# S5's direct terms placed by float32r matmuls of two parts, and the parameter work in seven parts per set

## The chip, the cores and the metric

The kernel runs on one core of one Trainium2 chip. The metric is the device time of one execution in microseconds (us), as the median of several runs. TensorE is called PE here (PEld is its weight load), VectorE is DVE, ScalarE is ACT, GpSimd is POOL and SyncE, which issues nearly all transfers, is SP. The granted TensorE clock is a share of 2.4 GHz: 1.00 is 2.4 GHz, 0.50 is 1.2 GHz.

## The reference, cut to what matters

Two two-layer networks run one after the other on 256 tokens of width 1024. Two stages matter here: the mixture of experts of the first network's second layer, and the S5 mixer that follows it.

```python
def hierarchical_moe(h, w_group, b_group, w_expert, b_expert, w_gate, w_up, w_down):   # 32 experts, top 2
    ...
        hb = jax.nn.silu(xb @ w_gate[e]) * (xb @ w_up[e])     # w_gate, w_up: 1024 x 512, float32
        return hb @ w_down[e]                                 # 512 x 1024
    ...

def s5_mixer(x, lam_re, lam_im, log_dt, b_re, b_im, c_re, c_im, d_skip, w_glu, w_out):
    ...
    a_re = mag * jnp.cos(li * dt)
    a_im = mag * jnp.sin(li * dt)
    ...
    bb_re = coef_re[..., None] * br - coef_im[..., None] * bi
    ...
    _, _, h_re, h_im = lax.associative_scan(
        _complex_linear_combine, (a_re_t, a_im_t, bu_re, bu_im), axis=1)
    y = (jnp.einsum('bsgp,gcp->bsgc', h_re, c_re.astype(f32))
         - jnp.einsum('bsgp,gcp->bsgc', h_im, c_im.astype(f32)))
    y = y + d_skip.astype(f32).reshape(N_GROUPS_2, SSM_GROUP) * u
    ...
```

S5 has 64 groups of 16 channels with 64 states. The kernel takes four time steps at once. What reaches an output from inputs of the same four steps does not go through the scan; these are the direct terms, products of C, powers of the decay and B, with `d_skip` on the diagonal.

## The kernel before

**The sets.** `moe(layer, ...)` goes through the 32 experts in eight sets of four (`qd` 0 to 7; set 1 is `qd` 0, set 8 is `qd` 7). All 25.2 MB of a set's float32 weights come from HBM through a ring of tiles of 1 MB (eight of them from set 3 of the second expert layer on), issued by SP in program order. A tile can be filled again only when the matmuls that read it are done. A set's order is: 16 tiles of gate and up weights in pairs (64 matmuls, L981), SiLU (L1000) and the product `hh` (L1001, DVE), four transposes (L1006), a copy to `ht` (L1008, ACT), and then 32 down matmuls (L1031) on eight tiles. The results are scaled into two float32r parts `y` (L1034 on ACT, L1035 on DVE) and spread back to the tokens (`back`, L1043), and DVE adds them (L1055). In every second set PE also gathers the next two sets' tokens (`gather`, L933). Set 7 adds six DVE operations on whole rows (L96 of `renew` and L989). Set 8 takes the down product in column pieces of 512, 256, 128 and 128 and makes the norm's moments as it goes (L308, L309); `norm_end` follows, with L331 on ACT as its first pass over the rows, and S5 begins.

**The parameter work.** S5's parameters need no tokens, so `s5_prepare` makes them beside the experts of the second expert layer. It is a generator; `moe` calls `next(stages)` at six places of each of the sets 1 to 7: after each half of the gate and up matmuls, after `hh`, after the second and the fourth quarter of the down matmuls, and after the adds. `stages` waits `NY` such calls, changes the ring, waits `N0` more and then runs `s5_prepare`. In set 8 whatever is left is run at once, ahead of the down matmuls. For each half of the groups (32) the parts are: `pair` of B (transposes L1368, copies `pr`), `bb` (L1388 to L1393), `W` (L1400 to L1404) with transposes L1410 to `BL`, `pair` of C (L1366), `CL` (L1419 to L1423) and then, twice, a `K` of 16 groups: matmuls L1432, copies L1434, the diagonal (L1436, L1438) and the placing. At the end come the tables `tab` of cosines and sines by doubling (L1470 to L1475, with `cmul` at L1242 to L1247, and L1483), which eight transfers (L96) copy into ring tiles.

**The placing.** `K` holds 16 x 64 numbers for each of 16 groups, in 16 partitions. Eight float32 matmuls (L1446) with slices of a 0/1 matrix `sel` of 16 rows move them to their place among 128 partitions; ACT copies the result to `KT` (L1449). The placing is done four times.

**What sets the order.** The program is written in this order, and the framework's scheduler then fixes one static order for every engine; buffers are handed over by semaphores. Each engine works through its own list strictly in order, so an instruction that waits holds up all behind it on its engine.

Of the kernel before, what the change touches and what calls it, by code (L numbers as in the profile page):

```python
# [8 lines left out]
F32 = mybir.dt.float32  # L9
F32R = mybir.dt.float32r  # L10
# [4 lines left out]
OP = mybir.AluOpType  # L15
# [20 lines left out]
GI = 1  # L36
NY = 12
NS = 1
# [6 lines left out]
EARLY = 1, 0  # L45
N0 = 4
FAST = (0, 1), (0, 1)
# [26 lines left out]
class Net:  # L74
# [707 lines left out]
    def moe(self, layer, rows, stages=()):  # L782
# [10 lines left out]
        with ExitStack() as ph:  # L793
# [170 lines left out]
            for qd in range(8):  # L964
# [57 lines left out]
                for i in range(4):  # L1022
                    v.tensor_copy(gs[32 * i:32 * i + 32], o[32 * i:32 * i + 32, i:i + 1])
                ob = [self.bank() for _ in range(2)]
                y = [[B.tile([128, 512], F32R, name=f"y{i}{j}", bufs=1) for j in range(2)] for i in range(2)]
# [223 lines left out]
    def s5_prepare(self):  # L1249
# [8 lines left out]
        with ExitStack() as es:  # L1258
# [80 lines left out]
            v.tensor_copy(dT, p[:16, :64])  # L1339
            sel = S.tile([16, 196], F32, name="sel")  # L1340
            nc.gpsimd.memset(sel, 0.0)
            v.tensor_copy(sel[:, 67:131:4], self.ident[:16, :16])
# [36 lines left out]
            for g0 in (0, H):  # L1379
# [46 lines left out]
                for q0 in range(g0 // 2, g0 // 2 + 16, 8):  # L1426
                    K = S.tile([16, 16, 4, 16], F32, name="K", tag="W")
                    for h8 in range(2):
                        p = self.bank("tp")
                        for g in range(8):  # L1430
# [6 lines left out]
                                    dT[:, q0 * 2:q0 * 2 + 16, None].to_broadcast([16, 16, 16]), op=OP.mult)  # L1437
                    v.tensor_tensor(K[:, :, 0, :], K[:, :, 0, :], dd, op=OP.add)  # L1438
                    yield
                    p = self.bank("tp")  # L1440
                    po = p.rearrange("p (q i c) -> p q i c", q=8, i=4)
                    Kg = K.rearrange("p (q g) n c -> p g q n c", g=2)
                    n = 0
                    for j in range(4):
                        for g in range(2):
                            nc.tensor.matmul(po[:, :, j:4, :], lhsT=sel[:, 67 - 64 * g - j:195 - 64 * g - j], rhs=Kg[:, g, :, 0:4 - j, :],  # L1446
                                             start=n == 0, stop=n == 7)
                            n += 1
                    a.copy(KT[:, q0:q0 + 8, :], p.rearrange("p (q m) -> p q m", q=8))  # L1449
# [15 lines left out]
            m = 1  # L1465
            while m < 64:
# [10 lines left out]
                if m < 64:  # L1477
                    w2 = [R.tile([128, H], F32, name=f"ww{m}{i}") for i in range(2)]
                    self.cmul(R, w2, wp, wp, [128, H], "cm")
                    wp = w2  # L1480
                else:
                    yield
# [498 lines left out]
    def stages0(self):  # L1981

        self.folds[1]()
        for _ in range(33):
            yield
# [66 lines left out]
```

## Time and profile before

| what | value |
|---|---|
| median of 3 runs (1853.5 to 1857.93) | 1855.04 us |
| profiled execution, its own time | 1861.03 us |
| its span, first to last instruction | 1859.1 us |
| mean granted TensorE clock | 0.938 |
| PE busy | 1583.7 us (85%) |
| DVE busy | 844.3 us (45%) |
| ACT busy | 500.0 us (27%) |
| read from HBM | 526.49 MB, 284 GB/s over the span |

The profile is one execution; it is 0.3% above the median. Busy shares are means over stages with different limits. The second expert layer lies between about 640 and 1230 us of the span, S5 after it.

### The profile page before, as it was taken

The page shows a single profiled execution, that of the slowest core. Times are in us where ns is not written, and L with a number is a line of the kernel's source. Part 1 is how long each engine was busy: PE and PEld are TensorE (multiplying, and loading weights), DVE is VectorE, ACT ScalarE, POOL GpSimd, SP SyncE. Part 2 cuts the span into 40 slices and gives each one's busy share as a digit, 9 for nine tenths or more (in the row PEclk, how much of TensorE's full clock was granted, in tenths as well). Part 3 has the DMA queues.
Part 4 walks back from the last instruction along what each step waited for, and adds up shares of the span by engine and source line. Part 5 has one row for each costly group of instructions (what it writes and reads, how often), then busy time and mean ns, then how long its engine had stood idle before and what let it go on. Part 6 is the DMA issues. An engine that isn't in the chain of part 4 may idle for free.

```text
span 1859.1 us, 24869 instructions
## 1 busy us (share of the span) xinstructions
PE 1583.7 (85%) x10036; PEld 1025.0 (55%) x10044; DVE 844.3 (45%) x1786; ACT 500.0 (27%) x807; POOL 123.8 (7%) x205
## 2 busy tenths in 40 slices
PE   7898777877786999787678779777999999999997
PEld 6773321322222995132223323256989998879997
DVE  5962011210312963014331442278775657785655
ACT  4721000000001632000110100033554445655441
POOL 3000000000100301000000010012100100300100
PEclk9988989998899999898997987879999999999999
DMA  9358999999999857999998999975745543435530
GB/s 305 148 210 354 420 420 420 419 420 420 410 420 384 308 211 293 420 411 390 409 377 344 375 369 362 367 141 176 252 138 199 185 142 108 159 136 182 185 111 23
DMA packets 150519, 535.55 MB, mean 288 GB/s; under 512 B 23141, under 2 KB 35686, under 8 KB 120698
## 3 DMA queue, kind: packets, MB, share of 16 engines
q1 hardware_dynamic: 148226, 532.04, 75.5%
q0 software_dynamic: 1856, 1.75, 0.4%
q8 instruction: 81, 1.33, 0.3%
q14 instruction: 44, 0.36, 0.1%
q10 hardware_dynamic: 312, 0.07, 0.0%
HBM read 526.49 MB, written 1.05 MB: 284 GB/s over the span
## 4 chain that ended last, share of the span: by engine, by line
PE 38%; DMA 13%; DVE 6%; ACT 2%; issue 1%; POOL 1%; SPq 0%; DVEq 0%; ACTq 0%; POOLq 0%
DMA raw<-in_moe_w_up 9%; PE mm L503 5%; PE mm L502 5%; PE mm L504 5%; PE mm L1031 4%; PE tp L503 3%; PE tp L502 3%; PE tp L504 3%; PE mm L981 3%; DMA raw<-in_moe_w_gate 2%; DMA raw<-in_moe_w_down 2%; PE tp L1446 2%; PE tp L933 1%; PE tp L1432 1%; DVE h L96 0%
## 5 line engine op out<-in xcount | busy, mean ns | idle before, releaser
L981 PE MATMUL mm<-raw,xg 128*32 128x512 f32 x2048 | 367.9, 684 | 152.7 <-DMA raw<-in_moe_w_up 86.9
L295 DVE TENSOR_TENSOR wlo<-raw,whi 128x1024 fp32r<-128x1024 f32 (+3 forms) x265 | 282.3, 1081 | 170.5 <-ACT whi L294 169.6
L981 PEld LDWEIGHTS mm<-raw,xg 128*32 128x32 f32 x2048 | 79.3, 121 | 424.7 <-DMA raw<-in_moe_w_up 153.4
L294 ACT CAST whi<-raw 128x1024 fp32r<-128x1024 f32 (+3 forms) x265 | 239.1, 919 | 244.9 <-PE mm L504 103.3
L1031 PE MATMUL mm<-raw,ht 128*32 128x512 f32 (+2 forms) x1120 | 205.8, 603 | 14.7 <-DMA raw<-in_moe_w_down 11.1
L1001 DVE TENSOR_TENSOR hh<-hh,mm 128x512 f32<-128x512 f32 x16 | 11.0, 688 | 423.4 <-PE mm L981 399.2
L502 PE MATMUL mm<-whi,f 128*128 128x512 f32 (+3 forms) x432 | 150.0, 347 | 0.0
L503 PE MATMUL mm<-wlo,f 128*128 128x512 f32 (+3 forms) x432 | 149.9, 347 | 0.0
L504 PE MATMUL mm<-whi,f 128*128 128x512 f32 (+3 forms) x432 | 149.1, 346 | 0.0
L503 PE MATMUL tp<-f,whi 128*128 128x256 f32 x512 | 145.1, 284 | 2.5 <-DVE f L419 2.5
L502 PE MATMUL tp<-f,whi 128*128 128x256 f32 x512 | 145.0, 284 | 0.4 <-ACT f L413 0.4
L504 PE MATMUL tp<-f,wlo 128*128 128x256 f32 x512 | 144.8, 283 | 0.0
L1031 PEld LDWEIGHTS mm<-raw,ht 128*32 128x32 f32 x1120 | 51.6, 117 | 124.4 <-issue 88.2
L1000 ACT ACTIVATE hh<-mm 128x512 f32<-128x512 f32 x16 | 9.6, 597 | 390.3 <-PE mm L981 359.9
L503 PEld LDWEIGHTS tp<-f,whi 128*128 128x128 f32 x512 | 98.3, 192 | 3.2 <-DVE f L419 3.2
L502 PEld LDWEIGHTS tp<-f,whi 128*128 128x128 f32 x512 | 98.1, 192 | 1.3 <-ACT f L413 0.9
L504 PEld LDWEIGHTS tp<-f,wlo 128*128 128x128 f32 x512 | 98.3, 192 | 0.0
L503 PE MATMUL mm<-xl,whi 128*128 128x272 f32 (+2 forms) x320 | 93.1, 292 | 0.9 <-DVE xl L419 0.5
L502 PE MATMUL mm<-xh,whi 128*128 128x272 f32 (+2 forms) x320 | 91.7, 292 | 0.6 <-ACT yg L674 0.4
L504 PE MATMUL mm<-xh,wlo 128*128 128x272 f32 (+2 forms) x320 | 92.0, 289 | 0.0
L502 PEld LDWEIGHTS mm<-whi,f 128*128 128x128 f32 x432 | 81.8, 189 | 10.3
L504 PEld LDWEIGHTS mm<-whi,f 128*128 128x128 f32 x432 | 81.5, 189 | 10.1 <-DVE f L419 0.2
(613 smaller groups left out, 2385.7 us busy)
## 6 DMA issues: line engine op xcount, KB each, us to landing
raw<-in_moe_w_gate SPq DMA_DIRECT2D x128, 1024.0 KB, 16.5
raw<-in_moe_w_up SPq DMA_DIRECT2D x128, 1024.0 KB, 19.9
raw<-in_moe_w_down SPq DMA_DIRECT2D x120, 1024.0 KB, 18.1
raw<-in_w_ff SPq DMA_DIRECT2D x64, 1024.0 KB, 5.0
raw<-in_sc_w_in SPq DMA_DIRECT2D x12, 1024.0 KB, 12.4
raw<-in_lru_w_in SPq DMA_DIRECT2D x8, 1024.0 KB, 13.9
raw<-in_ssm_w_glu SPq DMA_DIRECT2D x8, 1024.0 KB, 10.8
raw<-in_moe_w_down SPq DMA_DIRECT2D x12, 512.0 KB, 13.3
```

What stands on the lines that cost most here:

```text
L294: f(self.nc.scalar.copy)(hi, src)
L295: f(self.nc.vector.tensor_tensor)(lo, src, hi.bitcast(F32), op=OP.subtract)
L502: mm(out, lhsT=lh, rhs=rh, start=first, stop=False, skip_group_check=shared)
L503: mm(out, lhsT=lh, rhs=rl, start=False, stop=False, skip_group_check=shared)
L504: mm(out, lhsT=ll, rhs=rh, start=False, stop=last, skip_group_check=shared)
L933: nc.tensor.matmul(o, lhsT=hk[n][:, k, :], rhs=P[n], start=n == 0, stop=n == 1)
L981: nc.tensor.matmul(gu[m][i * 32:(i + 1) * 32, :], lhsT=xg[hf][:, k, c], rhs=wgu[hf * n + part][m][i][:, k % (4 // n), :], start=hf == 0 an ...
L1000: a.activation(hh, gu[0], AF.Silu)
L1001: v.tensor_tensor(hh, hh, gu[1], op=OP.mult)
L1031: nc.tensor.matmul(o[e * 32:(e + 1) * 32, :], lhsT=ht[:, j, e * 32:(e + 1) * 32], rhs=w[e], start=j == 0, stop=j == 3)
L1432: nc.tensor.matmul(p[:16, g * 64:(g + 1) * 64], lhsT=bb[0][:, gg - g0, :], rhs=CL[:, gg, 0:4, :].rearrange("p n c -> p (n c)"), start=True ...
L1446: nc.tensor.matmul(po[:, :, j:4, :], lhsT=sel[:, 67 - 64 * g - j:195 - 64 * g - j], rhs=Kg[:, g, :, 0:4 - j, :], start=n == 0, stop=n == 7)
```

## The change

1. `s5_prepare`'s placing. `sel` becomes float32r. `K` is copied to a float32r tile `Kh` by ACT; DVE makes the remainders `Kl = K - Kh` in two halves of eight groups. The eight float32 matmuls over all columns become eight float32r matmuls of `Kh` over all columns and two times eight of `Kl` over half the columns, all into the same PSUM bank: 24 instead of 8. The old placing read `K` itself, and the new one reads `Kh` and `Kl`.
2. `moe` calls `next(stages)` at a seventh place, ahead of the down matmuls, in both expert layers.
3. The counts are moved with it: `NY` 12 to 14 (the ring still changes at the start of set 3), `N0` 4 to 3 (`s5_prepare` begins ahead of set 3's down matmuls and not after the last of them), and the first layer's count 33 to 38.
4. The tables are made in three parts and not in one. With 32 calls left for `s5_prepare`, and not 26, its last K and all its tables come before set 8.

```diff
-NY = 12
+NY = 14
...
-N0 = 4
+N0 = 3
...
                 for i in range(4):
                     v.tensor_copy(gs[32 * i:32 * i + 32], o[32 * i:32 * i + 32, i:i + 1])
+                if qd < 7:
+                    next(stages, None)
                 ob = [self.bank() for _ in range(2)]
...
-            sel = S.tile([16, 196], F32, name="sel")
-            nc.gpsimd.memset(sel, 0.0)
+            sel = S.tile([16, 196], F32R, name="sel")
+            nc.gpsimd.memset(sel.bitcast(F32), 0.0)
...
+                    Kh = S.tile([16, 16, 4, 16], F32R, name="Kh")
+                    a.copy(Kh, K)
+                    parts = [(Kh, slice(0, 8))]
+                    for i, tag in enumerate(("pr1", "bb1")):
+                        Kl, e = S.tile([16, 8, 4, 16], F32R, name="Kl", tag=tag), slice(8 * i, 8 * i + 8)
+                        v.tensor_tensor(Kl, K[:, e], Kh[:, e].bitcast(F32), op=OP.subtract)
+                        parts.append((Kl, slice(4 * i, 4 * i + 4)))
                     yield
...
-                    Kg = K.rearrange("p (q g) n c -> p g q n c", g=2)
-                    n = 0
-                    for j in range(4):
-                        for g in range(2):
-                            nc.tensor.matmul(po[:, :, j:4, :], lhsT=sel[:, 67 - 64 * g - j:195 - 64 * g - j], rhs=Kg[:, g, :, 0:4 - j, :],
-                                             start=n == 0, stop=n == 7)
-                            n += 1
+                    for t, e in parts:
+                        t = t.rearrange("p (q g) n c -> p g q n c", g=2)
+                        for j in range(4):
+                            for g in range(2):
+                                nc.tensor.matmul(po[:, e, j:4, :], lhsT=sel[:, 67 - 64 * g - j:195 - 64 * g - j], rhs=t[:, g, :, 0:4 - j, :],
+                                                 start=e == slice(0, 8) and j + g == 0, stop=e.start == 4 and j + g == 4)
...
-                else:
+                if m > 8:
                     yield
...
-        for _ in range(33):
+        for _ in range(38):
```

Up to set 3 of the second expert layer every engine's list is the same as before, and SP's list of transfers is the same throughout. Line numbers in the changed kernel are 2 higher from L1024 on and 8 to 10 higher behind the placing: L1031 is L1033 there, L1446 is L1455, L1470 is L1478. Three places show what moved.

PE in set 5, before: a piece of the down matmuls (L1031, four at a time) with the products of K (L1432) and the placing (L1446) between them.

```order
L1432 MATMUL tp<-CL,bb_6918 16x64 x2
L1446 MATMUL tp<-K,sel 128x512 x2
L1031 MATMUL mm<-raw,ht 32x512 x4
L1446 MATMUL tp<-K,sel 128x8x48 x2
L1031 MATMUL mm<-raw,ht 32x512 x4
L1446 MATMUL tp<-K,sel 128x8x32 x2
L1446 MATMUL tp<-K,sel 128x8x16 x2
L1432 MATMUL tp<-CL,bb_6918 16x64 x14
L1031 MATMUL mm<-raw,ht 32x512 x4
L1432 MATMUL tp<-CL,bb_6918 16x64 x2
```

PE in set 5 of the changed kernel, from the last placing instructions to the end of the down matmuls (L1033), with the transposes for the second half's B (L1370) and BL (L1412).

```order
L1455 MATMUL tp<-Kl,sel 128x4x32 x2
L1455 MATMUL tp<-Kl,sel 128x4x16 x2
L1033 MATMUL mm<-raw,ht 32x512 x12
L1370 MATMUL tp<-ident,raw 128x32 x16
L1033 MATMUL mm<-raw,ht 32x512 x12
L1412 MATMUL tp<-ident,W 128x128 x8
L1033 MATMUL mm<-raw,ht 32x512 x4
L1412 MATMUL tp<-ident,W 128x128 x2
L1033 MATMUL mm<-raw,ht 32x512 x4
L1412 MATMUL tp<-ident,W 128x128 x6
```

Two placings with both their products stood among set 5's down matmuls; now one whole placing stands ahead of them and none among them. The other placings went to the end of set 4 and the start of set 5, into set 6's down matmuls, and into set 7's gate and up matmuls.

PE at set 8, before: the last placing stands between the small matmuls behind the transposes of `hh` and the first down matmuls.

```order
L1017 MATMUL tp<-gt,P_7662 128x4
L1446 MATMUL tp<-K,sel 128x512 x2
L1446 MATMUL tp<-K,sel 128x8x48 x2
L1446 MATMUL tp<-K,sel 128x8x32 x2
L1446 MATMUL tp<-K,sel 128x8x16 x2
L1031 MATMUL mm<-raw,ht 32x512 x16
L1031 MATMUL mm<-raw,ht 32x256 x2
```

PE at set 8 of the changed kernel, the same place.

```order
L1014 MATMUL tp<-ident,P_7830 128x128
L1017 MATMUL tp<-gt,P_7828 128x4
L1017 MATMUL tp<-gt,P_7830 128x4
L1033 MATMUL mm<-raw,ht 32x512 x16
L1033 MATMUL mm<-raw,ht 32x256 x2
L1045 MATMUL mm<-y_8372,pt 128x512 x2
```

Nothing stands between `hh` and the down matmuls of set 8 any more.

DVE in set 8, before: the last doubling of the tables, with set 8's second `y` (L1035) and its adds and moments (L308, L309) among them.

```order
L308 SCALAR_TENSOR_TENSOR h_64<-h_64,mm 128x512
L1471 TENSOR_TENSOR tt<-tab,ww_8273 128x1024
L1473 TENSOR_TENSOR tab<-tab,ww_8272 128x32x32
L1472 TENSOR_TENSOR tab<-tab,tt 128x32x32
L1035 SCALAR_TENSOR_TENSOR y_8181<-mm,gs,y_8180 128x256
L1474 TENSOR_TENSOR tt<-tab,ww_8273 128x1024
L309 BN_STATS bst_8341<-h_64 128x6
L1475 TENSOR_TENSOR tab<-tab,tt 128x32x32
L308 SCALAR_TENSOR_TENSOR h_65<-h_65,mm 128x512
L1483 TENSOR_SCALAR tab<-tab 128x2048
```

DVE in the changed kernel, where the tables end: the `hh` behind them (L1001) is that of set 7.

```order
L1481 TENSOR_TENSOR tab<-tab,ww_8152 128x32x32
L1479 TENSOR_TENSOR tt<-tab,ww_8153 128x1024
L1480 TENSOR_TENSOR tab<-tab,tt 128x32x32
L1482 TENSOR_TENSOR tt<-tab,ww_8153 128x1024
L1483 TENSOR_TENSOR tab<-tab,tt 128x32x32
L1491 TENSOR_SCALAR tab<-tab 128x2048
L1001 TENSOR_TENSOR hh<-hh,mm 128x512
L1020 CAST pt<-tp 128x256
```

All the tables, and set 7's six row operations ahead of them, are now in front of set 7's `hh` in DVE's list, and set 8's `hh`, `y` and moments have nothing of the parameter work among them.

## Rows read from the trace of the kernel before

**Rows 1.** Busy time by stretch: sets 4 to 7, cut at last up weights.

Columns: stretch, its length, then per engine busy us and (x instructions), the granted clock, the DMA share, GB/s.

```profile
912.80:979.30 66.50, 50.57 (x322) 21.62 (x322) 22.31 (x42) 8.55 (x15) 0.98 (x2) 0.97 0.99 386
979.30:1051.00 71.70, 61.02 (x322) 23.95 (x322) 19.60 (x37) 5.00 (x8) 0.00 (x0) 0.86 0.90 346
1051.00:1118.00 67.00, 52.66 (x322) 21.96 (x322) 29.26 (x46) 8.57 (x15) 6.94 (x8) 0.92 0.97 381
1118.00:1185.40 67.40, 54.67 (x294) 19.88 (x294) 9.66 (x19) 3.14 (x5) 0.00 (x0) 0.83 0.96 375
```

**Rows 2.** Busy time by stretch: where the transfers fall behind.

```profile
944.00:958.00 14.00, 9.03 (x56) 3.39 (x60) 12.48 (x21) 1.24 (x3) 0.00 (x0) 0.88 0.85 297
1006.00:1030.00 24.00, 24.00 (x140) 11.42 (x142) 8.33 (x13) 2.55 (x4) 0.00 (x0) 0.89 0.65 218
1090.00:1096.00 6.00, 6.00 (x42) 1.52 (x44) 5.83 (x8) 0.00 (x0) 2.69 (x2) 0.72 0.37 105
1144.00:1158.00 14.00, 13.63 (x96) 7.85 (x98) 5.85 (x9) 1.96 (x3) 0.00 (x0) 0.86 0.70 247
```

**Rows 3.** Groups of PE's instructions, 860 to 1230 us: records, busy, mean ns.

```profile
L1446 PE MATMUL tp<-K,sel 16*128 16x512 f32 (+3 forms) x64 | 29.7, 625 | 2.9 <-DVE K L1438 2.8 <-ACT ht L1008 0.2
...
L933 PE MATMUL tp<-P,h 128*128 128x256 f32 x64 | 18.3, 429 | 1.0 <-ACT BL L1412 1.0
L1432 PE MATMUL tp<-CL,bb 128*16 128x64 f32 x128 | 11.0, 256 | 0.3 <-ACT ht L1008 0.2
L1410 PE MATMUL tp<-ident,W 128*128 128x128 f32 x32 | 4.8, 283 | 0.3 <-ACT ht L1008 0.2
L1366 PE MATMUL tp<-ident,raw 32*64 32x32 f32 x128 | 4.7, 219 | 0.0
```

**Rows 4.** Timeline of PE in sets 1 and 4: start, duration, instruction.

```profile
742.07 8.08 PE L1031 MATMUL mm<-raw,ht 128*32 128x512 f32 x64 [0.19 <-ACT ht L1008]
...
917.38 1.91 PE L1031 MATMUL mm<-raw,ht 128*32 128x512 f32 x8
...
952.44 5.83 PE L981 MATMUL mm<-raw,xg 128*32 128x512 f32 x48
```

**Rows 5.** Timeline of DVE in sets 4 and 6.

```profile
944.82 0.69 DVE L1421 TENSOR_TENSOR CL<-pr,p 128x512 f32<-128x512 f32 x1
...
949.64 1.40 DVE L1035 SCALAR_TENSOR_TENSOR y<-mm,gs,y 128x512 fp32r<-128x512 f32 x2
...
1083.09 1.23 DVE L96 TENSOR_TENSOR h<-h,gb 128x1024 f32<-128x1024 f32 x1
```

**Rows 6.** Busy time by stretch: set 5's clock, and the end of weights.

```profile
960.00:990.00 30.00, 18.27 (x123) 6.13 (x124) 3.65 (x10) 1.18 (x2) 0.00 (x0) 1.00 1.03 410
992.00:1006.00 14.00, 14.00 (x37) 5.25 (x37) 0.00 (x0) 0.58 (x1) 0.00 (x0) 0.50 1.03 410
...
1207.00:1208.00 1.00, 0.00 (x0) 0.00 (x0) 1.00 (x4) 0.00 (x0) 0.00 (x0) 1.00 0.35 82
```

**Rows 7.** Timeline of all engines, from set 8's down matmuls into S5.

```profile
1191.21 7.78 PE L1446 MATMUL tp<-K,sel 16*128 16x512 f32 x16 [0.17 <-ACT ht L1008]
...
1199.38 0.23 DVE L1470 TENSOR_TENSOR tab<-tab,wp 128x32 f32<-128x32 f32 x1 [6.52 <-POOL tab L1463]
...
1204.57 0.69 ACT L1034 ACTIVATE y<-mm,gs 128x512 fp32r<-128x512 f32 x1 [4.96 <-DVE ww L1243]
...
1209.63 0.75 DVE L1035 SCALAR_TENSOR_TENSOR y<-mm,gs,y 128x512 fp32r<-128x512 f32 x1
...
1220.70 1.21 DVE L1483 TENSOR_SCALAR tab<-tab 128x2048 f32<-128x2048 f32 x1
...
1222.82 1.94 PE L1031 MATMUL mm<-raw,ht 128*32 128x128 f32 x32 [2.33 <-DVE y L1035]
...
1229.59 0.81 ACT L331 ACTIVATE h<-h,bmv 128x512 f32<-128x512 f32 x1 [4.32 <-DVE bmv L330]
...
1241.62 7.70 PE L1518 MATMUL mm<-f,place 128*128 128x512 f32 x32 [1.92 <-ACT f L413]
```

## Prediction, as put on record before the changed kernel ran

> **What bounds the kernel now.** The page shows PE at 85% and DVE at 45%, means over stages with different limits, so I went to the stage that the change touches, the second expert layer, and cut it by sets. [rows 1] cut it where a set's last up weights have landed (T4 = 912.8, T5 = 979.3, T6 = 1051.0, T7 = 1118.05, T8 = 1185.4). In the undisturbed stretch of [rows 6] the transfers run at 410 GB/s, and 25.17 MB at that rate take 61.4 us. The four steps took 66.5, 71.7, 67.0 and 67.4, so 27.0 us were lost. The same loss is seen where it happens, in [rows 2]: a stretch of length d at rate r loses d(1 - r/410), which gives 3.9, 11.2, 4.5 and 5.6, together 25.2 us. I use the second number. In three of the four stretches PE is busy all or nearly all the time: the ring's tiles are not given back because PE is not yet done. In the first PE waits, 9.0 of 14, and DVE is busy 12.5.
>
> How late PE may be follows from set 4. PE began to read set 5's first pair at 952.44, T4 + 39.6 [rows 4], and a pair takes about 2.0, so the tiles came back at T4 + 41.6 and the stretch lost 3.9. The transfers therefore run on if the first pair is given back by about T + 37.7.
>
> The second place is the tail. The last weights have all but landed at 1207.4 (82 GB/s in the last microsecond, [rows 6]), yet the last 32 down matmul records begin at 1222.82, and L331, the end of the norm's chain, at 1229.59 [rows 7]. Between them stand the last placing (7.78) ahead of the down matmuls, and the tables on DVE from 1199.38 to 1221.91, with set 8's `y` in their midst (1209.63, though ACT's half was ready at 1205.26).
>
> **The price of a placing.** Before: 29.7/4 = 7.4 us of PE [rows 3], mostly at half clock. After: 24 matmuls over 2560 + 2560 columns. The nearest float32r row is L1518, 32 matmuls of 512 columns in 7.70, 0.24 each [rows 7]; by columns that is 2.4 us. From above, the small products of L1432 (64 matmuls, 11.0/64 = 0.17 each, [rows 3]) give 24 x 0.17 = 4.1; and if float32r cost as much a column as the float32 placing, it would be 14.8. Below 2.4 nothing speaks for. I take 3 at full clock, since the columns per matmul lie between these rows, and 6 at half. New beside it: `Kh` on ACT, and two `Kl` on DVE, of about a `pr` or CL operation each (0.60 a piece by the eight CL operations from 944.82 to 949.64, [rows 5]), 2 us of a chain that only the `Kl` matmuls wait for.
>
> **The boundaries, set by set, at full clock.** From T to the first down matmul 4.6 us pass (917.38 in [rows 4]). Eight groups of four down matmuls in one run take 8.08, about 1.0 each; a group that stands alone takes 1.9 [rows 4]. So every piece of parameter work put between them costs 0.9 more than itself. From the start of the second-to-last `y` to the next pair's read it is 2.8 (949.64 to 952.44).
>
> Set 4 now holds the rest of BL (half of 4.8/2, 1.2), C's pair (4.7/2 = 2.35), the gather (18.3/2 = 9.15), one K's products (11.0/4 = 2.75), a third of a placing (1.2), and its down matmuls in six single groups and a double one (14.3). With 4.6 + 2.8 + 2.0 that is 40.4, so 2.7 us late against 3.9: C comes earlier, so its chain on DVE (three copies and twelve CL operations at 0.6, 9) is now under the gather, and no longer at the end.
>
> Set 5 held two placings and seven cuts at half clock. It now holds one placing (3, ahead of its down matmuls; its `Kl` stand ahead of `hh` on DVE, so PE does not wait for them), B's pair (2.35), BL (2.4) and four runs of down matmuls (11.6). That is 24 with the first 4.6; DVE's chain is longer: from the pair's end at T + 14, 2 for `pr`, then 24 operations of at most 0.6 (bb and two W), so `y` at T + 30.4, the next pair back at 35.2. It fits by 2.5 at full clock. I leave 1.5 us for the clock.
>
> Set 6 gets C's pair, K's products and a placing: 4.6 + 2.35, then CL until T + 17, products 2.75, K's copies and `Kh` 2, four single groups 7.6, Kl 1.7, a part of the gather 2, then 2.8 + 2.0: about 40, and part of the gather and the last placing stand among set 7's first gate and up matmuls. I take 3 late against 4.5.
>
> Set 7 has no parameter work in its down matmuls: 4.6 + 8.1 + 2.8 + 2.0 = 17.5, 20 us to spare against 37.7. That pays for DVE, whose list now has the six row operations (1.23 each, [rows 5]) and all tables (1199.38 to 1221.91, at most 22.5, some of it set 8's own, [rows 7]) ahead of set 7's `hh`. I put their start at T6 + 45, an estimate: the next pair back at 40, and some 5 for what is left of the gather. They end at T6 + 75 at the latest, when T7 is at T6 + 64.4 and `hh` is wanted at T7 + 2. So PE's transposes of `hh`, and all down matmuls behind them, wait up to 8.6 us, within the 20; 5.6 us are gained.
>
> After: 2.7 + 1.5 + 3 + 0 = 7.2 lost instead of 25.2, a gain of **18**. From one side all 25.2 come back; from the other, sets 5 and 6 at half clock lose about 10 and 8, which leaves a gain of 4.
>
> **The tail.** With the placing gone the down matmuls begin at 1191.2 (set 8's own scale) and not at 1199, a gain of 7.7, and without the tables `y` follows ACT's half (1205.26) and does not wait until 1209.63, 4.4: 12.1 together. Further waits for `y` would give more, but the weights land no earlier than T8 + 22.0, and from the last matmuls to L331 it is 6.8: T8 + 29.1 at best against T8 + 44.2, 15.1. Taken: **13.5**. What is late next is the last weights themselves. S5's first steps wait for the norm and for `tab`, whose transfers (behind the weights on SP) can now start when the weights end, so they stay hidden. Calls in the first layer cost nothing: its lists are the same, and the weights cover the ring's change as before.
>
> **Sum.** 18 + 13.5 = 31.5 us, from 1859.1 to 1827.6 of span. The execution profiled is 0.3% over the median, for which I keep the difference: 1855.04 - 31.5 = **1823.5**.
>
> **Rivals.** (a) The placings are cheap but the boundaries stay late, since the clock stays at half there: PE at 0.50 in 992 to 1006 while it was busy throughout, with the 16-row placing in its list, and 1.00 in 960 to 990 with 18.3 of 30 busy [rows 6]. The parameter work's many small pieces are still there, and if they bring the half clock as the placing did, only 0 to 8 of the 25.2 return: 1855 - 13.5 - 4 = 1837.5. The Trainium skill (TensorE: Matmul & The Clock Gate, section "HAM oscillation — how this bites in real kernels") has it that pauses of the matmuls for transfers send the clock to half, and by that a shorter placing would bring more of it, and the time would be this rival's; these two stretches show the reverse, so the rule adds nothing to its chance. (b) More comes back than I count, all stalls and the best tail: 1855 - 40 = 1815. (c) Slower: the half clock reaches through sets 4 to 6 whole. Then what PE does after T doubles: set 4 from 33 to 66, set 5 from 22 to 44, set 6 by 15; beyond T + 37.7 that is some 35, 8 and 17, 60 us lost instead of 25.2, and the tail at its lower end gives 12: 1878. It decides from a loss of 37 (25.2 + 12). Against it: in [rows 1] whole steps show 0.83 to 0.97. (d) The placing is no cheaper, as float32r costs what float32 does by column: 14.8 a placing instead of 3: sets 4, 5 and 6 are then late by 6.6, 9.3 and 14.8, 30.7 against 25.2, and with the tail the gain is 8, 1847. L1518's row speaks against it.
>
> **How the numbers follow.** Forecast (a gain of 22 to 37) 0.66; (b) 0.10; (a) 0.13; (d) 0.04; within 0.2%, which is about what a measurement of this kernel can tell from no change (1851.3 to 1858.7), 0.03; slower, by (c) or by DVE's list in set 7 passing its 20 us of room, 0.04. Range 1813 to 1840: it takes in (b) and (a) and leaves (c), (d) and no change out.
>
> **What would show it.** Right: 24 placing matmuls in about 3 us; T5 - T4 to T8 - T7 at 62 to 65, with no stretch like 1006 to 1030; set 7's `hh` some us after its last up matmul, with no dip of the transfers behind it; in set 8 the first down matmuls within 2 us of `hh`, and L331 at T8 + 29 to 32. Wrong: granted clock near 0.5 behind T5 and T6 with dips as before; the placing above 6; tables that end far behind T7; or S5 waiting for `tab`.

## The result, and the profile after

The changed kernel takes 1835.0 us (median of 4 runs, 1833.4 to 1836.7) against 1854.6 (4 runs, 1853.5 to 1857.9): a ratio of 0.9884, 95% interval 0.9856 to 0.9912. It is faster by 19.6 us where 31.5 were forecast; the time lies in the range, on its slower side. The execution profiled took 1836.65; its span is 1834.9, against 1859.1 before:

```profile
span 1834.9 us, 24946 instructions
```

The windows view of the changed kernel, first the steps T4 to T8 (T4 = 913.9, T5 = 980.0, T6 = 1044.6, T7 = 1110.5, T8 = 1172.0), then the stretches in which the transfers fall off. Columns: stretch, its length, busy time of PE, PE's weight loads, DVE, ACT and POOL, granted clock, DMA share, GB/s.

```profile
913.90:980.00 66.10, 56.60 (x402) 28.84 (x402) 24.59 (x45) 9.66 (x15) 0.98 (x2) 0.97 1.01 392
980.00:1044.60 64.60, 46.40 (x269) 18.70 (x269) 19.48 (x38) 7.08 (x12) 0.00 (x0) 0.87 0.97 379
1044.60:1110.50 65.90, 56.25 (x418) 29.82 (x418) 44.73 (x112) 9.27 (x14) 7.68 (x10) 1.00 1.00 391
1110.50:1172.00 61.50, 39.64 (x214) 10.91 (x215) 14.52 (x21) 2.56 (x4) 0.00 (x0) 0.89 1.03 408
952.00:966.00 14.00, 13.42 (x124) 7.59 (x122) 3.23 (x6) 1.63 (x2) 0.00 (x0) 1.00 0.93 348
1012.00:1024.00 12.00, 9.98 (x70) 4.06 (x72) 6.24 (x11) 2.34 (x4) 0.00 (x0) 1.00 0.74 242
1084.00:1100.00 16.00, 16.00 (x100) 8.68 (x103) 13.27 (x22) 2.76 (x4) 5.75 (x6) 1.00 0.90 334
```

Against [rows 1] the steps fell from 66.5, 71.7, 67.0 and 67.4 to 66.1, 64.6, 65.9 and 61.5. By d(1 - r/410), as for [rows 2], the last three lines lose 2.1, 4.9 and 3.0; behind T7 there is no such stretch.

The timeline of the changed kernel at set 7's `hh`, at the last up weights of set 8, and in the tail (start, length, engine, line; in brackets the wait ahead of it and what ended it):

```profile
1118.32 1.23 DVE L1491 TENSOR_SCALAR tab<-tab 128x2048 f32<-128x2048 f32 x1
1119.46 0.68 DVE L1001 TENSOR_TENSOR hh<-hh,mm 128x512 f32<-128x512 f32 x1
...
1171.97 1.91 PE L981 MATMUL mm<-raw,xg 128*32 128x512 f32 x12 [1.51 <-DMA raw<-in_moe_w_up]
...
1176.21 2.22 PE L1033 MATMUL mm<-raw,ht 128*32 128x512 f32 x4 [0.17 <-ACT ht L1008]
...
1182.81 6.42 PE L1033 MATMUL mm<-raw,ht 128*32 128x512 f32 x30 [1.66 <-DMA raw<-in_moe_w_down]
...
1203.43 0.81 ACT L331 ACTIVATE h<-h,bmv 128x512 f32<-128x512 f32 x1 [3.94 <-DVE bmv L330]
```

Set 7's `hh` stands behind the last of the tables, at T7 + 8.9. L331 comes at T8 + 31.5, before at T8 + 44.2 [rows 7]. The first down matmuls wait for `ht` alone, the later ones for their weights.

### The profile page after: what moved, and what is told of

Read it like the earlier page. It is cut to its first block, busy times and chain, and to the rows that moved or that the text cites. A ratio compares the mean times of both kernels' runs of the same rounds, so it can differ in the third digit from the quotient of the medians.

```text
span 1834.9 us, 24946 instructions
## 1 busy us (share of the span) xinstructions
PE 1550.8 (85%) x10068; PEld 1023.2 (56%) x10076; DVE 850.7 (46%) x1794; ACT 504.5 (27%) x811; POOL 123.7 (7%) x205
## 3 DMA queue, kind: packets, MB, share of 16 engines
q0 software_dynamic: 1856, 1.75, 0.4%
## 5 line engine op out<-in xcount | busy, mean ns | idle before, releaser
L981 PE MATMUL mm<-raw,xg 128*32 128x512 f32 x2048 | 360.7, 660 | 153.0 <-DMA raw<-in_moe_w_up 89.3
L1033 PE MATMUL mm<-raw,ht 128*32 128x512 f32 (+2 forms) x1120 | 193.8, 588 | 17.1 <-DMA raw<-in_moe_w_down 16.2
L1001 DVE TENSOR_TENSOR hh<-hh,mm 128x512 f32<-128x512 f32 x16 | 11.0, 687 | 412.1 <-PE mm L981 387.8
L1033 PEld LDWEIGHTS mm<-raw,ht 128*32 128x32 f32 x1120 | 47.8, 113 | 125.5 <-issue 82.9
## 6 DMA issues: line engine op xcount, KB each, us to landing
raw<-in_ssm_w_glu SPq DMA_DIRECT2D x8, 1024.0 KB, 10.8
```

Of the source, the lines that this page charges most:

```text
L981: nc.tensor.matmul(gu[m][i * 32:(i + 1) * 32, :], lhsT=xg[hf][:, k, c], rhs=wgu[hf * n + part][m][i][:, k % (4 // n), :], start=hf == 0 an ...
L1001: v.tensor_tensor(hh, hh, gu[1], op=OP.mult)
L1033: nc.tensor.matmul(o[e * 32:(e + 1) * 32, :], lhsT=ht[:, j, e * 32:(e + 1) * 32], rhs=w[e], start=j == 0, stop=j == 3)
```

## The experiments

For every profiled execution the same three numbers were read from its trace. **Loss**: over stretches of 2 us between the `hh` of one set and the next, the sum of 2(1 - r/410) where r is under 395 GB/s. **Half clock**: from the granted clock of the same stretches, from set 4's `hh` to set 8's. **Tail**: from set 8's `hh` to L331. The first two rows are two executions of one kernel, and so are the third, fourth and fifth of one order of instructions. Medians stand with the ratio to the kernel before on the same chip. The three numbers belong to the one execution profiled, which can lie several us off its kernel's median (moving alone: 1846.8 against 1841.9; control to B early: 1832.5 against 1838.1).

| kernel | median, ratio (95% interval) | loss of sets 4, 5, 6, 7 (sum) | half clock | tail |
|---|---|---|---|---|
| before | 1854.6 | 3.9, 11.3, 4.5, 5.9 (25.6) | 60 | 40.6 |
| before again | profiled execution 1847.5 | 5.0, 10.1, 4.5, 1.5 (21.1) | 48 | 38.5 |
| changed | 1835.0, 0.9884 (0.9856 to 0.9912) | 2.7, 4.9, 3.1, 0.1 (10.8) | 34 | 29.4 |
| changed, again | 1834.6, 0.9889 (0.9861 to 0.9916) | 2.5, 2.8, 8.9, 0.3 (14.5) | 67 | 27.5 |
| changed, tables held for set 8 | 1831.5, 0.9846 (0.9802 to 0.9890) | 2.9, 1.1, 3.6, 0.1 (7.7) | 27 | 29.5 |
| float32r placing alone | 1851.2, 0.9975 (0.9958 to 0.9992) | 4.9, 11.5, 5.1, 0.2 (21.7) | 51 | 37.5 |
| moving alone | 1841.9, 0.9926 (0.9897 to 0.9954) | 3.3, 6.3, 13.5, 0.2 (23.3) | 61 | 31.2 |
| upper part alone | 1834.1, 0.9879 (0.9853 to 0.9906) | 4.1, 1.3, 6.8, 0.2 (12.4) | 49 | 30.0 |
| dummy matmuls | 1831.6, 0.9854 (0.9819 to 0.9890) | 2.9, 1.9, 6.9, 0.2 (11.9) | 31 | 29.3 |
| N0 at 6 | 1840.8, 0.9904 (0.9871 to 0.9936) | 4.9, 0.2, 10.9, 0.2 (16.2) | 34 | 31.0 |
| N0 at 7 | 1846.2, 0.9940 (0.9915 to 0.9966) | 4.6, 10.2, 3.7, 2.7 (21.2) | 51 | 30.9 |
| B early | 1833.2, 0.9889 (0.9863 to 0.9915) | 2.8, 1.5, 4.9, 0.2 (9.4) | 27 | 30.6 |
| control to B early | 1838.1, 0.9923 (0.9893 to 0.9953) | 2.3, 4.8, 5.0, 0.1 (12.2) | 20 | 30.0 |
| B early, N0 at 2 | 1840.6, 0.9928 (0.9903 to 0.9954) | 15.6, 0.4, 2.2, 0.2 (18.4) | 41 | 29.5 |

**The two halves of the change.** First the float32r placing in the order of before:

```diff
-            sel = S.tile([16, 196], F32, name="sel")
+            sel = S.tile([16, 196], F32R, name="sel")
...
+                    Kh = S.tile([16, 16, 4, 16], F32R, name="Kh")
+                    a.copy(Kh, K)
...
```

> The kernel before with the float32r placing alone; calls, counts and tables as before. Theory (placing and moving gain in different places): a placing takes 3.8 us as in the changed kernel and not 7.4; the two placings in set 5 and the one in set 7 no longer hold up the next set's pairs, so the steps T5 to T6 and T7 to T8 (71.7 and 67.4) come to about 66 and 64, T4 to T5 and T6 to T7 stay at 66 to 67; the tail keeps its tables on DVE, whose end then binds, so T8 to L331 falls by no more than 4 (44.2 to 40 or more). Sum 10 to 13: about 1843, a ratio of 0.994. Rival 1 (the type of the matmuls is all): the steps come out as in the changed kernel and the tail too, 1835 to 1838. Rival 2 (the moving is all): the steps stay as before, 1851 or more.

It gains 0.25%, some 4 us: less than the theory's 10 to 13, and as little as its second rival (the moving is all, 1851 or more). The tail and set 7 gained little more than the second execution of before shows of itself, and set 5, with two placings, lost as much as ever. Its timeline and windows in set 5:

```profile
991.73 1.18 PE L1453 MATMUL tp<-Kh,sel 16*128 16x512 f32 x2 [2.45 <-ACT Kh L1440]
992.84 3.63 PE L1031 MATMUL mm<-raw,ht 128*32 128x512 f32 x8
```

```profile
990.00:1002.00 12.00, 10.27 (x27) 3.81 (x27) 2.16 (x5) 1.04 (x1) 0.00 (x0) 0.57 1.03 410
1006.00:1034.00 28.00, 25.58 (x166) 11.52 (x163) 14.93 (x24) 4.28 (x6) 0.00 (x0) 0.88 0.70 242
```

The shorter placing waits for its own new chain (`Kh`, 2.45), and the clock is at half from 992 to 1002 with no float32 placing in the list.

Then all the rest of the change with the float32 placing:

```diff
-                    Kh = S.tile([16, 16, 4, 16], F32R, name="Kh")
...
+                    Kg = K.rearrange("p (q g) n c -> p g q n c", g=2)
...
```

> The changed kernel with the float32 placing of before (8 matmuls, 7.4 us at full or half clock); the seventh call, the counts and the three parts of the tables as in the changed kernel. Theory: the tail gains all it gained in the changed kernel (T8 to L331 at 31 to 32, before 44.2), since no placing and no table is left in set 8; the boundaries gain little, for four placings cost 3.6 more each in sets 4 to 7, so T4 to T8 sums to 265 to 273 (258.1 in the changed kernel, 272.6 before). Time 1839 to 1847, a ratio of about 0.993. Rival 1 (the float32 placing brings half clock wherever it stands): granted clock near 0.5 behind each placing and T4 to T8 at 275 or more, 1850 or more. Rival 2 (moving is all): 1835 to 1837.

It comes out as the theory had it, 1841.9, T4 to T8 in 270.3, L331 at T8 + 33.2. The two halves add up to 17 (4 + 13) of the 20 us, with intervals of 3 and 5 us to either side. In the execution profiled, what float32r brings in the new order is mostly set 6, which loses 13.5 here at half clock; how much of that is the placing's is not shown, since this set of the changed kernel lost 3.1, 8.9 and 3.6 in three executions. The first of these windows is set 6's boundary, the second the stretch behind it; the rows are the first placing, at full clock:

```profile
1046.00:1070.00 24.00, 19.43 (x159) 10.21 (x152) 13.80 (x26) 1.78 (x3) 0.97 (x2) 0.66 1.03 409
1080.00:1114.00 34.00, 33.77 (x192) 16.76 (x191) 25.05 (x70) 4.11 (x7) 6.18 (x8) 0.90 0.73 251
```

```profile
943.18 1.12 PE L1448 MATMUL tp<-K,sel 16*128 16x512 f32 x2
...
946.07 1.77 PE L1448 MATMUL tp<-K,sel 16*128 16x512 f32 x4
...
950.79 1.99 PE L1448 MATMUL tp<-K,sel 16*128 16x384 f32 x8
...
954.56 0.48 PE L1448 MATMUL tp<-K,sel 16*128 16x128 f32 x2
```

That is 5.4 us in four pieces, not 7.4.

**The kernel before a second time.**

> The kernel before, unchanged, profiled a second time. The first profile's execution took 1861.03 us, 6.4 over the median of 1854.6, and the forecast took its terms from it. If that excess lay where the terms were read (sets 4 to 7 of the second expert layer, their half-clock stretches), the steps T4 to T8, 272.6 us in the first profile, come out some 4 to 6 us shorter here at a time near 1854 to 1856, the most of it in T5 to T6 (71.7). If the excess lay elsewhere, the steps sum to 272 +- 1.5 again and the rest of the program is shorter.

T4 to T8 took 268.2, 4.4 less, but not where this was expected: set 5 lost 10.1 again, set 7 1.5 and not 5.9. The tail from T8 was 40.5 and not 44.2, 2.1 of it by a placing that ran shorter. The window is set 7's dip (1.3 us lost, before 5.6 [rows 2]), the rows are the last placing (7.78 in [rows 7]) and L331.

```profile
1144.00:1150.00 6.00, 5.63 (x37) 2.21 (x32) 3.57 (x6) 1.37 (x2) 0.00 (x0) 1.00 0.95 323
```

```profile
1182.40 5.67 PE L1446 MATMUL tp<-K,sel 16*128 16x512 f32 x16 [0.17 <-ACT ht L1008]
...
1218.70 0.81 ACT L331 ACTIVATE h<-h,bmv 128x512 f32<-128x512 f32 x1 [4.32 <-DVE bmv L330]
```

So 8.1 us of what the forecast counted (4.4 and 3.7) are not in this execution. How much of it is the kernel's lies in between: the first execution is 6.4 us over its median, this one 7.8 under that of its chip (1855.2) and faster than all 18 runs of before there, so the average of the two is nearer to the kernel than either.

**The changed kernel a second time**, beside the last three variants:

> The changed kernel, unchanged, on the same chip as the three variants below: 1831 to 1836, ratio 0.985 to 0.989; T4 to T8 255 to 259, the loss of set 5 (stretches behind T5 under 410 GB/s) 3 to 5 us.

Time and set 5 (2.8) nearly as expected; T4 to T8 took longer (261.9), as set 6 lost 8.9 and not 3.1 with the same list of instructions. PE in set 6 of that execution, and windows of it:

```profile
1046.32 0.75 PE L1006 MATMUL tp<-ident,hh 128*128 128x128 f32 x4 [0.85 <-DVE hh L1001]
...
1050.39 6.25 PE L1033 MATMUL mm<-raw,ht 128*32 128x512 f32 x32
1059.97 3.47 PE L1434 MATMUL tp<-CL,bb 128*16 128x64 f32 x31 [3.32 <-DVE CL L1425]
```

```profile
1048.00:1056.00 8.00, 8.00 (x90) 3.77 (x90) 5.43 (x13) 1.20 (x2) 0.59 (x2) 0.57 1.03 407
...
1059.00:1066.00 7.00, 6.03 (x40) 4.29 (x40) 4.54 (x9) 1.04 (x1) 0.00 (x0) 0.51 1.03 408
```

The same place of the execution in the first section:

```profile
1044.00:1054.00 10.00, 7.63 (x106) 4.19 (x108) 4.07 (x10) 1.78 (x3) 0.97 (x2) 1.00 1.03 409
1054.00:1066.00 12.00, 8.42 (x65) 4.14 (x63) 10.92 (x19) 1.04 (x1) 0.00 (x0) 1.00 1.03 409
```

One set, one order, clock 1.00 or half: 3.1 or 8.9 us. Of the 15 falls to half clock that this second trace shows between 900 and 1200, 14 stand behind a pause of PE (for weights, `hh`, W or CL) and one behind work without a pause. But a pause is no sure sign of a fall: in the first trace, more than half of the 25 pauses of 1.4 us or more in the same stretch passed with no fall right behind them.

**What still holds sets 4 and 6.** The 16 matmuls of `Kl` and its two subtractions left out:

```diff
-                    for i, tag in enumerate(("pr1", "bb1")):
-                        Kl, e = S.tile([16, 8, 4, 16], F32R, name="Kl", tag=tag), slice(8 * i, 8 * i + 8)
...
```

> The changed kernel without the lower part: the two subtractions and the 16 matmuls of Kl are left out (the direct terms are those of the float32r-rounded K alone), so a placing has 8 matmuls, about 1.4 us, and not 24 in 3.8. Theory (what is still lost in sets 4 and 6 is PE's own parameter work, that between the next set's first pairs included): each of the two sets, that hold about two placings each, loses some 2 to 4 us less, T4 to T5 and T6 to T7 at 62 to 64 (66.2 and 66.0 in the changed kernel), time about 1829 to 1831, ratio 0.986. Rival (a price of the chain on DVE and of transfers, not of PE's work): the steps stay at 66, time 1834 to 1836, ratio 0.9884.

The time is the rival's: 0.9879, no other than the changed kernel's ratio, though the interval takes in the theory's 0.986 too. A placing takes 1.8 us here, 2 less, and sets 4 and 6 lost no less (4.1 and 6.8). The test is not a clean one: in set 6 the scheduler also put the second K's products ahead of set 7's first pair, and the clock was at half for 10 us ahead of that pair. What it suggests is that 2 us of PE at a boundary count for less than what the clock changes there from one execution to the next (3.1 or 8.9).

**Two that settled little of what they were for.** Tables held for set 8:

```diff
+            while not self.tables_now:
+                yield
             R = es.enter_context(self.pool("s5r", side="right"))
```

> The changed kernel, but the tables wait for set 8 as before, while the placings stay out of it: the tail's two parts apart. In the prediction the placing held 7.7 of the tail's gain and the tables 4.4. Theory 1 (that split): the first down matmuls of set 8 start within 2 us of hh as in the changed kernel, and T8 to L331 goes from 31.5 to 36, the time by 4 to 5 (1839 to 1840). Theory 2 (the tables bind once the placing is gone: 22.5 us on DVE from T8 + 7 at the earliest, and 7.7 from their end to L331): T8 to L331 at 37 or more, 1841 or more. Rival (DVE's list in set 7 was late and cost something): set 7's hh is now in time and T7 to T8 or T8 to T8 + hh shorter, which gives back 1 to 3 us: no slower than 1837.

The scheduler put the tables ahead of set 7's `hh` all the same (1093 to 1113 in its trace), so DVE's order is that of the changed kernel, and the run counts as a third execution of it. How the tail's gain divides between placing and tables stays open.

Dummy matmuls in the waits of the gate and up matmuls:

```diff
+                            if layer == 1 and hf and 3 <= qd:
+                                self.warm(0.65)
```

> The changed kernel with three dummy matmuls (0.65 us) behind each group of gate or up matmuls in the second half of sets 4 to 8, where PE waits for weights (pauses of 0.65 and 1.51 us in turn, 59% busy); nothing of the result hangs on them. Theory (the half clock at the sets' boundaries comes from PE's pauses ahead of them, not from what stands behind): the granted clock is 1.00 from T - 5 to T + 10, where it was 0.50 at 970 to 974, 980 to 984 and 988 to 993 in the changed kernel; the work behind T runs in half the time there, T4 to T8 falls from 258.1 to 252 to 256, the time to 1828 to 1833. Rival 1 (the clock falls with what stands behind T, the small pieces): the same stretches at 0.50, and the dummies cost nothing or up to 0.65 us a group where PE is late: 1835 to 1840. Rival 2: the clock stays up but the steps do not change, since DVE's and ACT's chains end last there: 1834 to 1836.

1831.6, but the run above, on the same chip and without dummies, has 1831.5. Among the gate and up matmuls no fall is left (908, 970, 980 and 1110 in the changed kernel's trace, 906, 1104 and 1134 in that of the run above); but one trace without dummies, that of the control to B early below, has only one there either (1034), so this is not shown to be their doing. Behind `hh` and behind waits for DVE (985, 998, 1046, 1056, 1114) the falls came as before. Two of them say something of the cause. The dummies (L105) fill the wait for `hh`, so PE has no pause over 0.11 us from 976.6 to the fall at 985, and none from 1040.6 to that at 1046. Ahead of the first stands the placing, ahead of the second the transposes of C's pair. PE at the first, and the clock ahead of the fall and in it:

```profile
978.41 0.82 PE L105 MATMUL mm<-busy 128*128 128x512 bf16 x2
...
980.76 1.50 PE L1457 MATMUL tp<-Kh,sel 16*128 16x512 f32 x8
982.10 1.94 PE L1457 MATMUL tp<-Kl,sel 16*128 16x256 f32 x16
```

```profile
974.00:984.70 10.70, 8.94 (x61) 5.32 (x65) 1.63 (x6) 1.17 (x2) 0.00 (x0) 1.00 1.02 408
984.70:988.30 3.60, 3.60 (x18) 0.81 (x12) 0.00 (x0) 0.00 (x0) 0.00 (x0) 0.53 1.03 411
```

So at these two boundaries the half clock does not come from pauses right ahead of it, against the theory. That leaves the mechanism of rival 1, what stands behind T, though its time did not come.

**Other places for the same work.** The start of the parameter work three and four calls later:

```diff
-N0 = 3
+N0 = 6
```

> The changed kernel with N0 at 6, not 3: the parameter work begins three calls later. Sets 4 and 6, which hold the gather too, have less of it (set 4 BL and C, as before; set 6 one BL, C and one K without its placing), set 5 has two Ks with their placings, set 7 one K with its placing; the tables stand between set 7's placing and set 8's hh on DVE. Theory (what sets 4 and 6 still lose, 4.8 and 4.6, is the sum of gather and parameter work in one boundary, while set 7 has 20 us of room): T4 to T5 66, T5 to T6 64 to 67, T6 to T7 63 to 64, T7 to T8 61.4 to 62, sum 255 to 258; T8 to L331 31 to 32; time 1831 to 1835. Rival (two Ks in one set bring back what that set lost before, whatever the placing costs): T5 to T6 at 70 to 72, sum 262 or more, 1839 or more.

> The same with N0 at 7: set 4 has one BL with the gather, and C among set 5's first gate and up matmuls; set 5 two Ks with their placings, the last of them and B among set 6's first matmuls; set 6 BL and C with the gather; set 7 two Ks with their placings ahead of and among its down matmuls, and the tables on DVE behind them. Theory (as for N0 at 6): T4 to T5 64, T5 to T6 65 to 68, T6 to T7 64, T7 to T8 62 to 63, sum 255 to 259, 1832 to 1836. Rival 1 (two Ks in one set): T5 to T6 and T7 to T8 at 70 and 64, 1840 or more. Rival 2 (the tables now end behind set 8's last up matmul): set 8's hh later than T8 + 4 and the tail longer than 33, 1838 or more.

Both are slower than the changed order on the same chip (1831.5). With N0 at 6, set 5 holds two Ks and loses 0.2, its boundary at full clock from T5 + 3.3 on, against the rival; set 6, which holds one K less than in the changed kernel but the transposes to a BL besides, loses 10.9 with 17 us at half clock. With N0 at 7 set 5 loses 10.2 with 20 us at half clock.

B a call earlier, its control, and the former with N0 at 2:

```diff
-                    if g0 == 0 and q0 == 8:
+                    if g0 == 0 and q0 == 0:
                         load("ssm_b_re_2", "ssm_b_im_2", 0, H)
-                    yield
+                    if g0 or q0 == 0:
+                        yield
```

```diff
-                yield
+                if g0 == 0:
+                    yield
                 v.tensor_tensor(bb[0], B1, bc(cf[0]), op=OP.mult)
```

> The changed kernel with the second half's B read a call earlier: its load is issued at the first K, and the call boundary between the second placing and B's transposes is taken out. B's 16 transposes now stand ahead of set 5's down matmuls, not behind the first 12 (order; 24 by the trace). All that follows comes one call earlier: C with set 5's last down matmuls, both Ks of the second half in set 6. Theory (set 5 is late because DVE gets B's pair only at T + 18 and works on it until T + 34, PE waiting 6.9 + 2.0 us for W): the first W is there at T + 18 and not T + 28, the next set's first pair is read by T + 36 instead of T + 39, set 5 loses 1 to 2 us and not 4.9; sets 4 and 6 lose what they lost (2.7 and 3). T4 to T8 2 to 4 us shorter than in the changed kernel. Rival (it is the sum of PE's work that is late, and C has come to it): set 5 loses 4 to 6 as before, no change in time or up to 3 us slower.

> The control to it: the changed kernel with the call boundary between the second half's B pair and bb taken out, B's transposes where they were. Everything behind bb comes one call earlier as in the kernel with B early, except B itself. Theory (B's late start is the cause in set 5): set 5 loses 4 to 5 as in the changed kernel, with C among set 6's first gate and up matmuls a little more; set 6 as in the kernel with B early; time as the changed kernel or up to 3 us slower. Rival (the shift of all that follows is what helps or hurts): time within 1 us of the kernel with B early.

> B early as above, and N0 at 2: B's transposes are now in set 5's gate and up matmuls, so DVE makes bb and the first W while PE waits for weights; set 5's down matmuls have only BL and C among them, set 4 the same as before plus more of the placings among set 5's first matmuls, set 6 two Ks with their placings and the gather. Theory (DVE's chain off the boundary): set 5 loses 0 to 1, pair read by T + 32; set 4 3 to 5, set 6 3 to 5; T4 to T8 as with B early or 2 shorter. Rival (two Ks in one set cost what they cost before and in the kernel with N0 at 6, 72): T6 to T7 at 69 to 72, time 1838 or more.

PE in set 5 with B early, then in the control:

```profile
987.03 1.97 PE L1370 MATMUL tp<-ident,raw 32*128 32x32 f32 x16
...
999.52 1.06 PE L1412 MATMUL tp<-ident,W 128*128 128x128 f32 x8 [2.63 <-DVE W L1406]
...
1015.40 7.06 PE L981 MATMUL mm<-raw,xg 128*32 128x512 f32 x62
```

```profile
991.40 1.94 PE L1370 MATMUL tp<-ident,raw 32*128 32x32 f32 x16
...
1003.77 1.94 PE L1413 MATMUL tp<-ident,W 128*128 128x128 f32 x8 [6.87 <-DVE W L1407]
...
1018.09 4.50 PE L981 MATMUL mm<-raw,xg 128*32 128x512 f32 x40
```

The first wait for W falls from 6.87 to 2.63, the second goes from 1.90 to 2.48, and set 5's loss falls from 4.8 to 1.5, with 14 us at half clock in both. That is what the theory says of this set, but it does not prove it: the changed kernel's own order, B's chain in its old place, lost 4.9, 2.8 and 1.1 there in three executions, and the control has C's pair between set 6's first gate and up matmuls besides. In time B early is the changed kernel (0.9889 both) and its control 5 us slower, with runs that overlap (1831.7 to 1835.8, 1832.5 to 1846.7). The third loses its gain in set 4 (15.6, 20 us at half clock). None of the variants clearly beats the changed kernel.

## Why the time fell into the range, and what was mis-sized

The direction and the places were right: the gain came at the boundaries of the last sets and in the tail, set 7's late `hh` cost nothing, and S5 waits for nothing new. On average over the executions profiled, set 5's loss fell by 7.8 us, set 7's by 3.5 and set 4's by 1.8; set 6 gained nothing (4.5 before, 5.2 after).

The size was not right. The gain of 19.6 lies under the 22 to 37 us to which the forecast gave 0.66, and the nearest of its times is that of rival (a), 1837.5; the range holds because it took that rival in. Its own signs are mixed: two of the four steps (66.1 and 65.9) are over the 62 to 65 asked for, and behind T5 there is half clock with a dip of the transfers (1012 to 1024, 242 GB/s), which was to be a sign of being wrong. Step by step:

- **The placing.** Predicted 3 us at full clock against 7.4. In set 6 the four pieces take 1.39 + 0.32 + 1.75 + 0.40 = 3.9, near the upper bound of 4.1; in one run at full clock (set 5 with the tables held, shown below, 980.67 to 983.95) it is 3.3:

```profile
1064.58 1.39 PE L1455 MATMUL tp<-Kh,sel 16*128 16x512 f32 x7 [0.58 <-ACT Kh L1442]
...
1067.74 0.32 PE L1455 MATMUL tp<-Kh,sel 16*128 16x128 f32 x1
1067.90 1.75 PE L1455 MATMUL tp<-Kl,sel 16*128 16x256 f32 x14
...
1071.42 0.40 PE L1455 MATMUL tp<-Kl,sel 16*128 16x64 f32 x2
```

  The larger error is on the other side: 29.7/4 of [rows 3] was, as the forecast itself says, mostly a price at half clock, and it was set against one at full. The float32 placing takes 5.4 at full, so at one clock and in four pieces float32r saves 1.5 and not 4.4.
- **The boundaries.** Predicted losses 2.7, 1.5, 3 and 0; the profile has 2.7 (0.66 at 930 to 932 included), 4.9, 3.1 and 0.1, the average of the three executions of this order 2.7, 2.9, 5.2 and 0.2. The term that failed in this profile is set 5's, where the forecast left 1.5 us for the clock. PE in set 5:

```profile
985.79 1.55 PE L1455 MATMUL tp<-Kh,sel 16*128 16x512 f32 x8
987.14 3.56 PE L1455 MATMUL tp<-Kl,sel 16*128 16x256 f32 x16
...
995.80 1.95 PE L1370 MATMUL tp<-ident,raw 32*128 32x32 f32 x16
...
1008.16 1.94 PE L1412 MATMUL tp<-ident,W 128*128 128x128 f32 x8 [6.86 <-DVE W L1406]
...
1019.26 7.07 PE L981 MATMUL mm<-raw,xg 128*32 128x512 f32 x64
```

  B's pair ends at T5 + 17.7, not + 14; the two W stand in line behind it, and the next pair is read from T5 + 39.2, where the forecast had that at 33.2 (and the pair back at 35.2). The clock is at half from 980 to 984, 987 to 994 and 1004 to 1011. The same list in the run with the tables held, where T5 is at 976.5 and half clock ahead of B's pair lasts 3.4 us and not 10.2:

```profile
980.67 1.50 PE L1455 MATMUL tp<-Kh,sel 16*128 16x512 f32 x8
982.01 1.94 PE L1455 MATMUL tp<-Kl,sel 16*128 16x256 f32 x16
...
989.13 1.94 PE L1370 MATMUL tp<-ident,raw 32*128 32x32 f32 x16
...
1012.61 7.07 PE L981 MATMUL mm<-raw,xg 128*32 128x512 f32 x64
```

  Here B's pair ends at T5 + 14.6, the next pair is read from T5 + 36.1, and the set loses 1.1. So some 3 of the 6 us by which that read came late are the clock's. How the other 3 divide between the clock and the chain of DVE behind B's pair is not shown; B early fits the chain, but its 1.5 us lie within what this order lost without it. For set 6 the forecast's own terms add up to 37.9 and not to about 40, so the 3 us taken there had little behind them; the two executions at full clock there lost 3.1 and 3.6, the one at half 8.9.
- **The tail.** Predicted 29 to 32 behind T8, measured 31.5: a gain of 12.7 on this pair of profiles, where 13.5 were taken. Against both executions of before it is 10.8 (from set 8's `hh`, tails of 39.6 and 28.8 on average). The best case of T8 + 29.1 is 28.8 by its own terms (22.0 and 6.8).
- **The sum was made against one execution.** The profile of before took 1861.0 where its median was 1854.6, and most of set 7's 5.6 us (1.5 in the other execution) and a part of the tail were that execution's. On average over the executions profiled, the losses fell by 12.4 (23.4 to 11.0) and the tail by 10.8, together 23.2. Behind L331 2.5 us went the other way (628.2 before, 630.7 after), though no instruction changed there, and ahead of set 4's `hh` 1.2 (913.4 and 914.6). With that it is 19.5, about the time measured. Whether the 2.5 is more than chance is open: two executions of one kernel differ by as much there (626.9 and 629.6 before, 628.8 and 631.8 after). Of the 11.9 us by which the forecast was too high, the boundaries are 5.6 (18 against 12.4), the tail 2.7, and these two stretches 3.7.
- **Rival (a)** had the mechanism that was underrated: the clock stays at half at boundaries whatever the placing costs. The forecast held against it that in [rows 6] the clock was at half while PE was busy and at full while it paused. What the two windows hide is what came ahead. In the kernel before, the clock falls at 991.0, just behind a pause of 1.38:

```profile
989.87 2.65 PE L1446 MATMUL tp<-K,sel 16*128 16x512 f32 x4 [1.38 <-DVE K L1438]
```

  The trace of the float32r placing alone shows a pause of 2.45 at the same place and then the half clock, with the small float32r matmuls in the list, and 14 of 15 falls in the second trace of the changed kernel stand behind pauses. The Trainium skill (TensorE: Matmul & The Clock Gate, section "HAM oscillation — how this bites in real kernels") has the rule that pauses of the matmuls for transfers bring the half clock; the forecast set it aside. These rows agree with it in part: a pause, for DVE as well as for transfers, stands ahead of nearly every fall, but many pauses as long pass without one, and some falls come without. In the fourteen traces ten falls between 900 and 1200 have no pause right ahead of them; nine stand in or shortly behind a placing, the tenth (with dummies, at 1046) behind transposes of C's pair. So the forecast's reading, that the parameter work's small matmuls bring the half clock, is not refuted by these runs, and float32r did not end it; most placings brought no fall, and what decides it stays open. The full price of this rival did not come, since the new order has room behind T7 (13 us at half clock between T7 and the next pair's read, 0.1 lost) and, in some executions, in set 5.

## To carry over

Price an instruction at the clock of its stretch, and compare the two forms at the same clock: 7.4 against 3.9 was 5.4 against 3.9. Where the clock moves from execution to execution, profile the kernel twice before summing its losses, since single boundaries changed by 4 to 6 us with nothing changed in the program. An experiment on one boundary needs the same care: a loss of 1.5 us proves nothing where the unchanged order lost between 1.1 and 4.9. Moving work off the boundaries and out of the tail gained more than making it cheaper did: 13 against 4 us, each taken alone.

## What the runs showed of the hardware

- The same list of instructions had the granted clock at 1.00 or at about half in set 6, and the set lost 3.1 or 8.9 us; over sets 4 to 7 the time at half clock lay between 27 and 67 us in three executions.
- A float32 placing from 16 rows (2 x 1280 columns) took 5.4 us in pieces at full clock, the float32r one with twice the columns and three times the matmuls 3.9, and 3.3 in one run.
- With dummy matmuls in waits of 0.65 and 1.51 us, the one trace taken shows no fall of the clock among the gate and up matmuls, and five behind `hh` and the waits for DVE. Traces without dummies have from one (control to B early) to eight (the changed kernel's second) among the gate and up matmuls, so an effect of the dummies is not shown.
- PE pauses of 1.4 us or more stood ahead of most falls to half clock, but more than half of the 25 that the changed kernel's first trace has between 900 and 1200 us brought none. Ten falls in fourteen traces came with PE busy: nine in or shortly behind the matmuls from 16 rows that make a placing, one behind 32x64 transposes.
